# Hybrid decoder step on one core: first gated outputs loaded one unit ahead, branch weights walked forth and back

## Chip, core, metric

One Trainium2 chip, one core of it. The metric is the device time of one execution in microseconds (us), the median of the runs shown. All arithmetic is float32; products are made from two fp32r halves (a high part and the rest).

## What is computed

One layer for a prompt of 2048 positions and a sample group of 8 x 8 positions, D_MODEL 1024. A combined input projection feeds two branches, a windowed attention and a gated linear attention (GLA). The part that matters here is how the branch outputs are joined:

```python
h = rms_norm(x, norm_g) * (1.0 + scale) + shift
q_a, k_a, v_a, z_a, q_g, k_g, v_g, lr_g, z_g, m_a, m_g = split_proj(h @ w_in)
...
o_a = attention(...) * silu(z_a)                     # 512 channels
o_g = rms_norm(gla(...), gla_norm_g) * silu(z_g)     # 512 channels
merged = sigmoid(m_a) * (o_a @ w_branch_att) + sigmoid(m_g) * (o_g @ w_branch_gla)
y = x + gate * (merged @ w_out)
```

## The kernel before

Three phases follow each other. Sixteen prompt tiles of 128 positions and one sample tile of 64 are the units of position; weights and activations have their contraction rows on the 128 partitions, in chunks (`r`, `d`) of 128 rows.

**phase_a1** makes the modulation, the normed input, the attention branch, and stores the attention outputs per tile in DRAM (`oa_dram`).

**phase_gla** (L589) runs the rest of the input projection as 16 weight units `u`, over three blocks of columns `bi` (384, 384 and 288 columns; the loops stand at L920 and L927). A unit loads its raw weights (`raw`, L613, pool `r`, 7 buffers), splits each into halves (`halves`, L606: a cast on ACT, a subtraction on DVE, pool `w`, 7 buffers) and makes 7 products of 12 matmuls (L941) into banks a to d. Between them the GLA steps (`step`, L913) are worked off. In block 1 each unit also splits one piece of the branch weights and stores it in DRAM (`branch_weights`, L652: tile `wl`, store `sw<-wl`). Some units also prepare the *first gated outputs*, those of the first block of the last phase: `first_outputs(zc)` (L896) for eight chunks `zc` of channels. It loads the gate path `z` and four tiles of branch output `or`, takes the sigmoid on ACT (L903), multiplies twice on DVE (L904, L905), splits (`o0w`) and stores (`o<-o0w`, L907). Chunks 0 to 3 stand in units 9, 11, 13 and 15 of block 1, chunks 4 to 7 in units 0 to 3 of block 2; loads and products stand together at the beginning of a unit. `z`, `or` and the sigmoid `sg` are buffers of the pool `r`.

**phase_out** (L965) has four blocks `bi` of tiles: 512, 512, 512 and 576 positions, the last with the sample tile. In each block:

- the gated outputs `o[zc]` (trace name `d_o`) are made for 8 chunks from `z` and `orw` (L1014 to L1026); for block 0 they are loaded ready;
- for each of 8 chunks `dj` of output channels, two gate paths `s` are loaded and put through the sigmoid (L1039 to L1044), two products of 12 matmuls are made (`product`, L580, matmuls at L585, trace name `q`), and DVE joins and splits the result into `m` (L1054 to L1060, `split` L990). Two chunks `dj` share one *branch unit*, 2 MB of split weights, loaded by `unit` (L974) in two halves (`u_b<-sw`, L977) into one of two buffers, even units into `wp0`, odd ones into `wp1`. Units are taken in the order 0, 1, 2, 3 in each block, so each block loads four;
- the output projection: 8 groups of 24 matmuls (L1078, trace name `e`; the sample tile at L60), summed over `r` = 0 to 7 in that order, then gate, residual and store.

In block 0 the output weights `wo` are loaded as well, as 16 pieces (`pieces`, L994, three buffers `x`), each split by ACT and DVE (L991, L992). They are tied behind the branch units on their queue by `issue_after` (L1033).

All these transfers are issued by SP, in one order. The order on each engine and on SP's queue is not the program's: a scheduler fixes it when the program is built, with the program's order as priority and a simulated time line for what is ready (`schedule_with_timeline_sim=True`). At run time each engine and each queue goes strictly in that fixed order. So the last products of one block and the first ones of the next can be mixed on PE.

Of the kernel before, what the change touches and what calls it, by code (L numbers as in the profile page):

```python
# [9 lines left out]
F32R = mybir.dt.float32r  # L10
# [7 lines left out]
P = 128  # L18
D = 1024
NC = 8  # L20
# [16 lines left out]
def f(ap):  # L37
    return ap.bitcast(F32)
# [550 lines left out]
def phase_gla(k, dp):  # L589
# [4 lines left out]
    tc, nc, I, O = k.tc, k.nc, k.i, k.o  # L594
    k.og_dram = {}
    with ExitStack() as es:
# [16 lines left out]
        def raw(name, src=None):  # L613
            r = rp.tile([P, 4, P], F32, tag="r", name=name)
            if src is not None:
                nc.sync.dma_start(r, src)
            return r
# [277 lines left out]

        def first_outputs(zc):  # L896

            z, o, sg = (raw(f"{n}0_{zc}") for n in ("z", "or", "sg"))
            flat = lambda t: t.rearrange("p a b -> p (a b)")
            nc.sync.dma_start(flat(z), zm[zc][:, 0, 0:512])  # L900
            for n, t in enumerate(k.blocks[0]):
                nc.sync.dma_start(o[:, n], (k.oa_dram if zc < 4 else k.og_dram)[t][:, zc % 4])
            nc.scalar.activation(sg, z, AF.Sigmoid)  # L903
            nc.vector.tensor_tensor(z, z, o, op=ALU.mult)  # L904
            nc.vector.tensor_tensor(z, z, sg, op=ALU.mult)  # L905
            k.o0[zc] = dp.tile([P, 2, 512], F32R, tag=f"o0_{zc}", name=f"o0_{zc}")
            nc.sync.dma_start(f(k.o0[zc]), f(halves(z, f"o0w{zc}")).rearrange("p a b c -> p a (b c)"))  # L907

        k.o0 = {}
        lags = ((store, 5), (output, 4), (levels, 3), (operands, 2), (decay, 0), (sums, 1), (fetch, 1))  # L910
        steps = iter(range(len(k.order2) + 5))

        def step():  # L913
            n = next(steps, None)
            for fn, lag in lags if n is not None else ():
                if 0 <= n - lag < len(k.order2):
                    fn(k.order2[n - lag])

        step()
        for bi, (c0, c1) in enumerate(SB):  # L920
            N = c1 - c0
            w, X = unit(bi, 0) if bi == 0 else None, [None] * 7
            for p in ORDER:
                X[p] = xp.tile([P, 2, 4, 384], F32R, tag=f"x{p}", name=f"x{p}_{bi}")[:, :, :, :N]
                nc.sync.dma_start(f(X[p]), f(k.xd[bi][p]))
            at = range(0, 12, 2) if bi < 2 else (0, 1, 2, 4, 5, 6, 8, 9, 10)
            for u in range(16):  # L927
                if u - 4 in at:
                    step()
                if bi == 1:  # L930
                    branch_weights(u)
                if (bi == 1 and u in (9, 11, 13, 15)) or (bi == 2 and u < 4):
                    first_outputs(u // 2 - 4 if bi == 1 else u + 4)
                w = unit(bi, u) if bi or u else w
                bank = {b: ps_d.tile([P, 512], F32, tag=b, name=f"{b}{bi}_{u}")[:, :N] for b in "abcd"}
                oc = [ep.tile([P, 2, 384], F32, tag="oc", name=f"oc{n}_{bi}_{u}")[:, :, :N] for n in range(2)]
                t = [up.tile([P, 384], F32, tag="u", name=f"u{n}_{bi}_{u}")[:, :N] for n in range(3)]
                for p, b, wt in zip(ORDER, "abcdacd", w):
                    for d in range(4):
                        for n, (x, y) in enumerate(((0, 0), (0, 1), (1, 0))):  # L940
                            nc.tensor.matmul(bank[b], wt[:, x, d], X[p][:, y, d], start=(p > 3 or p == 0) and d == 0 and n == 0,  # L941
                                             stop=(d == 3 and n == 2), skip_group_check=True)
                    if p == 0:
                        nc.scalar.copy(t[0], bank["a"])
                    elif p == 5:
                        nc.vector.tensor_tensor(t[0], bank["b"], t[0], op=ALU.add)
                    elif p == 4:
                        nc.scalar.copy(t[1], bank["c"])  # L948
                    elif p == 6:
                        nc.vector.tensor_tensor(t[2], bank["d"], t[0], op=ALU.add)  # L950
                        nc.gpsimd.tensor_tensor(oc[1][:, 1], t[2], t[1], op=ALU.add)  # L951
                    elif p == 1:
                        nc.scalar.copy(oc[0][:, 0], bank["a"])  # L953
                    elif p == 2:
                        nc.vector.tensor_tensor(oc[1][:, 0], bank["c"], t[0], op=ALU.add)
                    else:
                        nc.vector.tensor_tensor(oc[0][:, 1], bank["d"], t[0], op=ALU.add)
                for n in range(2):
                    dst = qkv[2 * u + n] if u < 4 else zm[2 * (u - 4) + n]
                    nc.sync.dma_start(dst[:, :, c0:c1], oc[n])  # L960
# [4 lines left out]
def phase_out(k):  # L965

    tc, nc, I, O = k.tc, k.nc, k.i, k.o
    with ExitStack() as es:
        tp = lambda name, bufs, **kw: es.enter_context(tc.tile_pool(name=name, bufs=bufs, reuse_waits="tile", **kw))

        wop, mp_, wp1, sp, wp0, op = tp("dewo", 1), tp("dem", 1), tp("dew1", 1), tp("des", 2), tp("dew0", 1), tp("deo", 1)
        pse, psl = tp("depa", 3, space=PSUM), tp("depb", 5, space=PSUM)

        def unit(key):  # L974
            w = (wp0, wp1)[int(key[-1]) % 2].tile([P, 2, NC, 256], F32R, tag="w", name="u" + key)
            for n, r in enumerate((slice(0, 4), slice(4, 8))):
                ins = nc.sync.dma_start(f(w[:, :, r]), f(k.split[int(key[-1])][:, :, r]))  # L977
                if key == "0_b0":
                    outputs(4 * n)
            return w[:, 0], w[:, 1], ins  # L980

        def outputs(zc0):

            for zc in range(zc0, zc0 + 4):
                o0.append(op.tile([P, 2, NB], F32R, tag=f"o{zc}", name=f"d_o0_{zc}"))
                last.append(nc.sync.dma_start(f(o0[zc][:, :, :512]), f(k.o0[zc])))
# [17 lines left out]
        for bi in range(len(k.blocks)):  # L1004
# [4 lines left out]
            o = [op.tile([P, 2, NB], F32R, tag=f"o{zc}", name=f"d_o{bi}_{zc}") for zc in range(8)] if bi else o0  # L1009
# [4 lines left out]
            for zc in range(8) if bi else ():  # L1014
                od = k.oa_dram if zc < 4 else k.og_dram
                z = sp.tile([P, NB], F32, tag="z", name=f"z{bi}_{zc}")
# [5 lines left out]
                sg = sp.tile([P, NB], F32, tag="sg", name=f"sg{bi}_{zc}", bufs=1)  # L1022
# [1 line left out]
                nc.vector.tensor_tensor(z[:, :N], z[:, :N], orw[:, :N], op=ALU.mult)  # L1024
                nc.vector.tensor_tensor(sg[:, :N], sg[:, :N], z[:, :N], op=ALU.mult)
                split(o[zc][:, 0, :N], o[zc][:, 1, :N], sg[:, :N])  # L1026
            for dj in range(8):
                if dj % 2 == 0 and (bi or dj):
                    with tc.issue_after(last[-1].ins) if bi == 0 else nullcontext():
                        wb = unit(f"{bi}_b{dj // 2}")  # L1030
                if bi == 0 and dj in (4, 6):
                    for e in (dj - 4, dj - 3):
                        with tc.issue_after(wb[2].ins):  # L1033
                            pieces(wo[:, :, :, e * 256:e * 256 + 256], I["w_o"][e], f"o{e}")
                if bi == 0 and dj == 7:
                    gate = wop.tile([P, D], F32, tag="gate", name="gate")
                    nc.sync.dma_start(gate, k.gates[:P])
                sm = []
                for s in range(2):  # L1039
                    t = sp.tile([P, NB], F32, tag=f"s{s}", name=f"s{s}_{bi}_{dj}")  # L1040
                    for o0, hf, c0, n in at:
                        nc.sync.dma_start(t[:, o0:o0 + n], zm[8 + 2 * dj + s][:, hf, c0:c0 + n])
                    nc.scalar.activation(t[:, :N], t[:, :N], AF.Sigmoid)  # L1043
                    sm.append(t)  # L1044
                sums = []
                for s in range(2):
                    ps = [psl.tile([P, 512], F32, tag="ps", name=f"q{s}{bi}_{dj}_{u}") for u in range(len(spl))]
                    rows = list(range(4 * s, 4 * s + 4))
                    product(nc, ps, spl, wb, dj % 2 * P, rows, o, rows)
                    sums.append(ps)  # L1050
                for u, (s0, s1) in enumerate(spl):
                    n = s1 - s0
                    sa, sg = sm[0][:, s0:s1], sm[1][:, s0:s1]
                    nc.vector.tensor_tensor(sa, sums[0][u][:, :n], sa, op=ALU.mult)  # L1054
                    nc.vector.tensor_tensor(sg, sums[1][u][:, :n], sg, op=ALU.mult)
                    nc.vector.tensor_tensor(sa, sa, sg, op=ALU.add)
                    e = min(s1, np_)
                    split(mp[:, 0, dj, s0:e], mp[:, 1, dj, s0:e], sa[:, :e - s0])
                    if s1 > np_:
                        split(ms[:, dj, 0], ms[:, dj, 1], sa[:, np_ - s0:n])  # L1060
# [196 lines left out]
```

## Time and profile before

| | |
|---|---|
| median of 3 runs | 1628.81 us |
| the runs | 1638.41, 1628.81, 1628.66 us |
| the profiled execution | 1636.97 us, its span 1635.2 us (1.8 us lie around it) |
| mean granted TensorE clock in it | 0.969 |
| DMA | 382.17 MB, mean 234 GB/s |

A span begins and ends with the first and last instruction seen. PE is TensorE's matmuls, PEld its weight loads, DVE VectorE, ACT ScalarE, POOL GpSimd, SPq the queue of the engine that issues the transfers. A granted clock of 1.0 is 2.4 GHz, 0.5 is 1.2 GHz. In a time line the last bracket is the idle time of the engine before the instruction and what ended it.

### The profile page before, as it was taken

What the parts mean: (1) busy time and instruction counts of PE and PEld (TensorE: products, weight loads), DVE (VectorE), ACT (ScalarE), POOL (GpSimd) and SP (SyncE); (2) the same over time, 40 slices, a digit from 0 to 9 for tenths busy, and PEclk for the clock granted to TensorE, in tenths of its full rate; (3) what the DMA queues carried; (4) which work ended last, traced back from release to release, by engine and by line L of the source; (5) the groups of instructions that cost most, each with busy time, mean ns of one, the idle gap of its engine ahead of it and who ended that gap; (6) DMA issues with size and microseconds to landing.
All of it is one profiled execution on the core that took longest, in us unless ns stands there. A gap on an engine that the chain in (4) does not pass through costs nothing.

```text
span 1635.2 us, 26988 instructions
## 1 busy us (share of the span) xinstructions
PE 1547.5 (95%) x9528; PEld 1349.5 (83%) x9528; DVE 1032.7 (63%) x2168; ACT 695.9 (43%) x1618; POOL 467.5 (29%) x553
## 2 busy tenths in 40 slices
PE   7789999989989999999999999999999889999998
PEld 5666666657989999899989998998898568888997
DVE  5886878764586877554666667677562653646452
ACT  3676856644433443333344445454232421313120
POOL 1895774652555444111111111124110000000000
PEclk9988999988999999899999999999999989999999
DMA  9875473566776566999667789966569976876633
GB/s 376 257 229 150 142 254 86 152 211 264 246 249 228 187 211 208 383 302 282 223 218 244 248 284 363 326 198 180 192 227 346 299 236 204 266 241 213 206 113 103
DMA packets 288283, 382.17 MB, mean 234 GB/s; under 512 B 37569, under 2 KB 196178, under 8 KB 284820
## 3 DMA queue, kind: packets, MB, share of 16 engines
q1 hardware_dynamic: 285700, 376.13, 69.7%
q10 hardware_dynamic: 2448, 4.33, 0.7%
q8 instruction: 75, 1.23, 0.3%
q14 instruction: 60, 0.49, 0.1%
HBM read 257.30 MB, written 123.08 MB: 233 GB/s over the span
## 4 chain that ended last, share of the span: by engine, by line
PE 43%; DMA 7%; DVE 5%; ACT 2%; issue 1%; SPq 1%; POOL 0%; ACTq 0%; DVEq 0%; POOLq 0%
PE e L1078 10%; PE q L585 9%; PE c L941 5%; PE d L941 5%; PE a L941 5%; PE b L941 2%; PE g_l L798 2%; DMA wo<-in_w_o 2%; DMA sw<-wl 1%; DVE KQ L750 1%; DMA o<-o0w 1%; DMA u_b<-sw 1%; DVE ATp L804 1%; DVE w L610 1%; DMA s<-zm 1%
## 5 line engine op out<-in xcount | busy, mean ns | idle before, releaser
L610 DVE TENSOR_TENSOR w<-r,w 128x512 fp32r<-128x512 f32 x208 | 158.7, 766 | 100.4 <-ACT w L609 91.4
L941 PE MATMUL c<-x,w 128*128 128x384 f32 (+1 forms) x1152 | 211.2, 329 | 6.5 <-ACT u L948 6.5
L941 PE MATMUL d<-x,w 128*128 128x384 f32 (+1 forms) x1152 | 205.9, 326 | 7.7 <-DVE u L950 7.7
L941 PE MATMUL a<-x,w 128*128 128x384 f32 (+1 forms) x1152 | 207.4, 325 | 0.2 <-ACT oc L953 0.2
L585 PE MATMUL q<-d_o,u_b 128*128 128x512 f32 (+1 forms) x960 | 189.6, 358 | 13.2 <-ACT d_o L991 9.6
L941 PEld LDWEIGHTS c<-x,w 128*128 128x128 f32 x1152 | 189.6, 192 | 11.1 <-ACT u L948 8.8
L941 PEld LDWEIGHTS d<-x,w 128*128 128x128 f32 x1152 | 188.9, 190 | 11.1 <-DVE u L950 8.6
L585 PEld LDWEIGHTS q<-d_o,u_b 128*128 128x128 f32 x960 | 161.3, 191 | 40.5 <-ACT d_o L991 11.6
L609 ACT CAST w<-r 128x512 fp32r<-128x512 f32 x208 | 127.4, 621 | 151.3 <-DMA sw<-wl 40.6
L941 PEld LDWEIGHTS a<-x,w 128*128 128x128 f32 x1152 | 185.5, 188 | 3.5 <-issue 1.3
L1078 PE MATMUL e<-wo,d_m 128*128 128x512 f32 x768 | 177.6, 392 | 2.8 <-ACT wo L991 2.6
L1078 PEld LDWEIGHTS e<-wo,d_m 128*128 128x128 f32 x768 | 144.7, 189 | 34.5 <-ACT wo L991 3.4
L951 POOL TENSOR_TENSOR oc<-u,u 128x384 f32<-128x384 f32 (+1 forms) x48 | 55.9, 1165 | 337.0 <-DVE u L950 169.5
L304 PE MATMUL pd<-whi,hs 128*128 128x512 f32 (+1 forms) x512 | 143.6, 361 | 7.0 <-DVE hs L242 4.3
L304 PEld LDWEIGHTS pd<-whi,hs 128*128 128x128 f32 x512 | 92.4, 196 | 26.2 <-DVE hs L242 4.5
L941 PE MATMUL b<-x,w 128*128 128x384 f32 (+1 forms) x576 | 105.5, 323 | 1.1 <-ACT w L609 1.1
L941 PEld LDWEIGHTS b<-x,w 128*128 128x128 f32 x576 | 93.3, 188 | 1.9 <-ACT w L609 1.4
L304 PE MATMUL pd<-wlo,hs 128*128 128x512 f32 (+1 forms) x256 | 91.7, 360 | 0.0
L375 ACT ACTIVATE sm<-sm,nm,rs 128x256 f32<-128x256 f32 (+1 forms) x128 | 74.5, 587 | 8.2 <-DVE nm L371 7.8
L750 DVE TENSOR_TENSOR KQ<-KQ,M 128x512 f32<-128x512 f32 (+2 forms) x115 | 71.8, 625 | 0.0
L804 DVE COPY_PREDICATED ATp<-maskp,g_l 128x256 f32<-128x256 int32 x112 | 58.4, 522 | 16.6 <-PE g_l L798 14.9
L1043 ACT ACTIVATE s<-s 128x512 f32<-128x512 f32 (+1 forms) x64 | 40.6, 645 | 65.1 <-DMA s<-zm 63.3
(252 smaller groups left out, 2611.4 us busy)
## 6 DMA issues: line engine op xcount, KB each, us to landing
r<-in_w_x SPq DMA_DIRECT2D x160, 256.0 KB
w<-tx SPq DMA_DIRECT2D x64, 512.0 KB
u_b<-sw SPq DMA_DIRECT2D x32, 1024.0 KB
x<-xd SPq DMA_DIRECT2D x14, 1536.0 KB
zm<-oc SPq DMA_DIRECT2D x48, 384.0 KB
xd<-sx SPq DMA_DIRECT2D x32, 512.0 KB
tx<-w SPq DMA_DIRECT2D x32, 512.0 KB
r<-tw SPq DMA_DIRECT2D x64, 256.0 KB
```

What stands on the lines that cost most here:

```text
L304: nc.tensor.matmul(pd[u][:T, :hi - lo], hs[:, d // 4, a, d % 4, :T], (whi, wlo)[b][:, d, lo:hi], start=(d == 0 and n == 0), stop=(d == NC ...
L375: nc.scalar.activation(sm[:, h, :w], sm[:, h, :w], AF.Exp, scale=0.125 if rq is None else rs[:, h:h + 1], bias=nm[:, h:h + 1], accum_out=d ...
L585: nc.tensor.matmul(ps[u][:, :s1 - s0], w[a][:, r, cs:cs + P], x[xr[n0]][:, b, s0:s1], start=(n0 == 0 and n == 0), stop=(n0 == len(rows) - ...
L609: nc.scalar.copy(w[:, 0], src)
L610: nc.vector.tensor_tensor(w[:, 1], src, f(w[:, 0]), op=ALU.subtract)
L750: nc.vector.tensor_tensor(out.rearrange("p a (n m) -> p a n m", m=m), x.rearrange("p a (n m) -> p a n m", m=m), M[r, b, at[n]:at[n + 1]].u ...
L798: nc.tensor.matmul(pl[:T, r, j, l - l0, :H], KQ[rr, l, j] if l else c["kT"][rr, j, :T], KQ[rr, l, 2 + j].rearrange("p (n s m) -> p n s m", ...
L804: nc.vector.copy_predicated(g.AT[:T].rearrange("p h (n s m) -> p h n s m", s=2, m=m)[:, :, :, 1, :], g.mask[:T, l, :].rearrange("p (n m) - ...
L941: nc.tensor.matmul(bank[b], wt[:, x, d], X[p][:, y, d], start=(p > 3 or p == 0) and d == 0 and n == 0, stop=(d == 3 and n == 2), skip_grou ...
L951: nc.gpsimd.tensor_tensor(oc[1][:, 1], t[2], t[1], op=ALU.add)
L1043: nc.scalar.activation(t[:, :N], t[:, :N], AF.Sigmoid)
L1078: nc.tensor.matmul(ps, mp[:, a, r, o0:o0 + T], wo[:, b, r, cs], start=(r == 0 and n == 0), stop=(r == 7 and n == 2))
```

## The change

First outputs become a generator: the loads of a chunk are issued in units 8, 10, 12, 14 of block 1 and 0 to 3 of block 2, its products follow in the next unit. So chunks 0 to 3 load one unit sooner and are multiplied where they were, and chunks 4 to 7 load where they did and are multiplied one unit later. In phase_out `unit` remembers what each of the two buffers holds and hands it out again; even blocks take `dj` as 0, 1, ... 7, odd blocks as 6, 7, 4, 5, 2, 3, 0, 1.

```diff
@@ -895,18 +895,20 @@
 
         def first_outputs(zc):
 
-            z, o, sg = (raw(f"{n}0_{zc}") for n in ("z", "or", "sg"))
+            z, o = (raw(f"{n}0_{zc}") for n in ("z", "or"))
             flat = lambda t: t.rearrange("p a b -> p (a b)")
             nc.sync.dma_start(flat(z), zm[zc][:, 0, 0:512])
             for n, t in enumerate(k.blocks[0]):
                 nc.sync.dma_start(o[:, n], (k.oa_dram if zc < 4 else k.og_dram)[t][:, zc % 4])
+            yield
+            sg = raw(f"sg0_{zc}")
             nc.scalar.activation(sg, z, AF.Sigmoid)
             nc.vector.tensor_tensor(z, z, o, op=ALU.mult)
             nc.vector.tensor_tensor(z, z, sg, op=ALU.mult)
             k.o0[zc] = dp.tile([P, 2, 512], F32R, tag=f"o0_{zc}", name=f"o0_{zc}")
             nc.sync.dma_start(f(k.o0[zc]), f(halves(z, f"o0w{zc}")).rearrange("p a b c -> p a (b c)"))
 
-        k.o0 = {}
+        k.o0, outs = {}, {}
         lags = ((store, 5), (output, 4), (levels, 3), (operands, 2), (decay, 0), (sums, 1), (fetch, 1))
         steps = iter(range(len(k.order2) + 5))
 
@@ -929,8 +931,11 @@
                     step()
                 if bi == 1:
                     branch_weights(u)
-                if (bi == 1 and u in (9, 11, 13, 15)) or (bi == 2 and u < 4):
-                    first_outputs(u // 2 - 4 if bi == 1 else u + 4)
+
+                for n in (u - 1, u):
+                    if (bi == 1 and n in (8, 10, 12, 14)) or (bi == 2 and n in (0, 1, 2, 3)):
+                        zc = n // 2 - 4 if bi == 1 else n + 4
+                        next(outs.setdefault(zc, first_outputs(zc)), None)
                 w = unit(bi, u) if bi or u else w
                 bank = {b: ps_d.tile([P, 512], F32, tag=b, name=f"{b}{bi}_{u}")[:, :N] for b in "abcd"}
                 oc = [ep.tile([P, 2, 384], F32, tag="oc", name=f"oc{n}_{bi}_{u}")[:, :, :N] for n in range(2)]
@@ -971,13 +976,19 @@
         wop, mp_, wp1, sp, wp0, op = tp("dewo", 1), tp("dem", 1), tp("dew1", 1), tp("des", 2), tp("dew0", 1), tp("deo", 1)
         pse, psl = tp("depa", 3, space=PSUM), tp("depb", 5, space=PSUM)
 
+        held = {}
+
         def unit(key):
-            w = (wp0, wp1)[int(key[-1]) % 2].tile([P, 2, NC, 256], F32R, tag="w", name="u" + key)
-            for n, r in enumerate((slice(0, 4), slice(4, 8))):
-                ins = nc.sync.dma_start(f(w[:, :, r]), f(k.split[int(key[-1])][:, :, r]))
+            n = int(key[-1])
+            if held.get(n % 2, (None,))[0] == n:
+                return held[n % 2][1]
+            w = (wp0, wp1)[n % 2].tile([P, 2, NC, 256], F32R, tag="w", name="u" + key)
+            for h, r in enumerate((slice(0, 4), slice(4, 8))):
+                ins = nc.sync.dma_start(f(w[:, :, r]), f(k.split[n][:, :, r]))
                 if key == "0_b0":
-                    outputs(4 * n)
-            return w[:, 0], w[:, 1], ins
+                    outputs(4 * h)
+            held[n % 2] = n, (w[:, 0], w[:, 1], ins)
+            return held[n % 2][1]
 
         def outputs(zc0):
 
@@ -1024,7 +1035,9 @@
                 nc.vector.tensor_tensor(z[:, :N], z[:, :N], orw[:, :N], op=ALU.mult)
                 nc.vector.tensor_tensor(sg[:, :N], sg[:, :N], z[:, :N], op=ALU.mult)
                 split(o[zc][:, 0, :N], o[zc][:, 1, :N], sg[:, :N])
-            for dj in range(8):
+
+            for n in range(8):
+                dj = (n // 2 if bi % 2 == 0 else 3 - n // 2) * 2 + n % 2
                 if dj % 2 == 0 and (bi or dj):
                     with tc.issue_after(last[-1].ins) if bi == 0 else nullcontext():
                         wb = unit(f"{bi}_b{dj // 2}")
```

## Rows read from the trace of the kernel before

**Rows 1.** Page: busy time and share of the span, by engine

```profile
PE 1547.5 (95%) x9528; PEld 1349.5 (83%) x9528; DVE 1032.7 (63%) x2168; ACT 695.9 (43%) x1618; POOL 467.5 (29%) x553
```

**Rows 2.** Windows: stretch, length, busy us (count) per engine, PEclk, DMA share, GB/s

```profile
1243.10:1282.51 39.41, 36.76 (x158) 29.23 (x158) 14.85 (x24) 12.77 (x20) 0.00 (x0) 1.00 0.97 327
1282.51:1323.78 41.27, 28.49 (x92) 19.98 (x92) 28.44 (x45) 20.74 (x36) 0.00 (x0) 0.75 0.90 291
1441.81:1485.33 43.52, 43.52 (x193) 36.04 (x193) 22.32 (x33) 12.34 (x20) 0.00 (x0) 1.00 0.79 264
800.00:960.00 160.00, 151.50 (x1052) 144.35 (x1051) 103.22 (x215) 76.66 (x161) 25.26 (x29) 1.00 0.77 245
```

**Rows 3.** Chain of waits, 1230 to 1330 us: start, length, what

```profile
1283.28 11.43 DMA u_b<-sw
...
1299.36 8.90 DMA wo<-in_w_o
...
1308.32 7.00 DMA s<-zm
```

**Rows 4.** Waits of PE, 1280 to 1325 us: total, times, longest

```profile
PE q L585 <- ACT d_o L991: 9.6, 3, 3.8
PE e L1078 <- ACT wo L991: 2.6, 2, 1.7
```

**Rows 5.** DMA issues over the whole span: count, KB each

```profile
u_b<-sw SPq DMA_DIRECT2D x32, 1024.0 KB
```

**Rows 6.** Time line of SP's queue, 1195 to 1335 us

```profile
1282.70 1.18 SPq L977 DMA_DIRECT2D u_b<-sw  x2
1283.97 3.06 SPq L998 DMA_DIRECT2D wo<-in_w_o  x3
...
1307.61 0.52 SPq L977 DMA_DIRECT2D u_b<-sw  x1
...
1320.13 0.38 SPq L998 DMA_DIRECT2D wo<-in_w_o  x1
```

**Rows 7.** Time line of PE, 960 to 1000 us: the first unit of block 2

```profile
984.37 1.12 PE L823 MATMUL g_s<-g_v,kd 128*64 128x128 f32 x8 [2.01 <-ACT g_oT L891]
985.43 2.40 PE L798 MATMUL g_l<-KQ 64*128 64x64 f32 x20
...
988.52 2.94 PE L941 MATMUL c<-x,w 128*128 128x288 f32 x12
...
993.09 1.33 PE L798 MATMUL g_l<-KQ 64*128 64x64 f32 x18
...
997.34 1.84 PE L941 MATMUL c<-x,w 128*128 128x288 f32 x12
```

**Rows 8.** Waits of ACT, 640 to 1240 us

```profile
ACT w L609 <- DMA sw<-wl: 40.6, 10, 6.4
...
ACT L903 <- DMA z<-zm: 5.2, 1, 5.2
```

**Rows 9.** Waits of PE, 800 to 1240 us

```profile
PE c L941 <- ACT u L948: 5.8, 6, 1.8
```

**Rows 10.** Time line at the end of the last block's products

```profile
1579.84 6.53 PE L60 MATMUL e<-wo,d_m 128*128 128x512 f32 x28
...
1579.91 0.82 DVE L1055 TENSOR_TENSOR s<-q,s 128x288 f32<-128x288 f32 x2 [2.38 <-PE q L585]
...
1581.65 0.90 DVE L992 TENSOR_TENSOR d_m<-s,d_m 128x288 fp32r<-128x288 f32 x3 [0.19 <-ACT d_m L991]
```

**Rows 11.** Chain of waits of the whole span: a raw weight load; a unit's products

```profile
973.54 9.47 DMA r<-in_w_x
...
1000.76 1.58 PE b L941 x12
```

**Rows 12.** Page, groups: the two steps that free a raw buffer

```profile
L610 DVE TENSOR_TENSOR w<-r,w 128x512 fp32r<-128x512 f32 x208 | 158.7, 766 | 100.4 <-ACT w L609 91.4
...
L609 ACT CAST w<-r 128x512 fp32r<-128x512 f32 x208 | 127.4, 621 | 151.3 <-DMA sw<-wl 40.6
```

## Prediction

> **What bounds the kernel now.** I read the page first, then windows over the whole span, then the chain of waits and the waits of PE where a window showed PE idle. PE is busy 95% of the span, DVE 63% [rows 1]; so PE sets the end, and an edit is worth what it takes out of the 88 us in which PE is idle (1635.2 - 1547.5), or out of the time in which PE runs at the lower clock. Two of the places that the change touches have such losses.
>
> The first is the passage into the last phase. In a stretch without any loss 192 matmuls take 43.52 us, 0.2267 us each (the row counts 193, with one cut by its edge) [rows 2]. From 1282.51 to 1323.78 us PE makes only 92 in 41.27 us [rows 2]. At 0.2267 they are 20.9 us, so 20.4 us are lost: 12.8 idle (41.27 - 28.49) and 7.6 to a granted clock of 0.75 over the stretch, a mixture of its two levels that comes with the idle time. In the 39.41 us before it 158 matmuls would take 35.8, a loss of 3.6. In both stretches the DMA share is 0.90 to 0.97, at 291 and 327 GB/s: the transfers are the limit, not DVE (28.44 of 41.27) [rows 2]. The chain of waits goes through them: 11.43 us for a branch unit, 8.90 for a piece of `wo`, 7.00 for a gate path [rows 3]. PE itself waits for operands of block 1 (9.6 us) and for split pieces of `wo` (2.6) [rows 4]. After 1324 us it runs without a gap to the tail.
>
> The second is the first outputs. In block 1's half from 800 to 960 us PE is idle 8.5 us (160.00 - 151.50) [rows 2]; at the first unit of block 2 one wait of 2.01 us is followed by a spell at the lower clock [rows 7].
>
> **The change, part by part.** *Branch units kept.* Before, four units of two halves in each of four blocks make 32 loads of 1024 KB [rows 5]. After, blocks 1 to 3 find the two units that they begin with in place and load two: 8 + 3 x 4 = 20 loads. Of the twelve that go, eight belong to the starts of blocks 2 and 3, and there PE has no gap to give (as in the stretch at 1441.81, clock 1.00, DMA 0.79 [rows 2]): nothing gained. Four, the loads of block 1's first two units, are issued from 1282.70 to 1307.61 us [rows 6], inside the stretch that loses. They are 4.19 MB; at its 291 GB/s that is 14.4 us of a queue that is nearly full. The chain holds one of them with 11.43 us [rows 3]. The gain can't be more than the 20.4 us lost there. From below: the ten last pieces of `wo`, issued from 1283.97 to 1320.13 us [rows 6], go through three buffers, each with a landing, a cast and a subtraction, and these steps stay; if that cycle is what holds PE, only the transfers' competition goes, and it may be nothing. I take 12, next to the row of the chain, a little under the bytes' 14.4, because something is late next: the pieces of `wo`, then block 1's `d_o`.
>
> By the Trainium skill, page "DMA: Bandwidth & Descriptors", section "Anatomy of one DMA", a transfer costs about 2.0 us fixed (measured there for the software-generated path) plus its bytes at 436 GB/s: an estimate of 2.6 us for a piece of 256 KB. The trace has 8.90 us for one [rows 3], so most of it would be queueing, which the change removes; by that rule the pieces would stop being late, which is the second rival below.
>
> *Odd blocks backwards.* The number of products is the same. But the output projection sums over `r` from 0, and in blocks 1 and 3 the chunks 0 and 1 now come last, so it meets the fresh result at its second step, where before it had 28 matmuls (6.53 us in the last block) of older chunks to make first [rows 10]. The result of the last chunk is ready 2.64 us after the products end (1579.91 to 1581.65 + 0.90) [rows 10]. What still covers it are the `r` = 0 matmuls of the three groups that have a PSUM buffer: in block 3 two groups of the sample tile with 2 and one of 3, 7 x 0.2267 = 1.6 us, so 1.0 is exposed. In block 1, three groups of 3 give 2.0 us; nearly all is covered. Bounds: 0 and 2.64 in each. I take +1 in all.
>
> *First outputs.* No instruction is added; loads and products are set apart. At the first unit of block 2 ACT stood 5.2 us before the sigmoid until `z` had landed [rows 8], behind it in ACT's queue waited the copy `g_oT`, and PE waited 2.01 us for that. Then 20 matmuls took 2.40 us, where later 18 took 1.33, and 12 took 2.94 against 1.84 [rows 7]; PE lost 2.0 + 0.9 + 1.1 = 4.0 us there. With the sigmoid one unit later `z` has long landed. What is late next is the raw weights under a full DMA; I take 3 of the 4. In block 1 PE waited six times, 5.8 us, for ACT's copy `u` [rows 9]; ACT was held by casts that wait until a store of `wl` has landed (ten times, up to 6.4 us) [rows 8]. These stores share the DMA engines with the loads of `z` and `or`, issued right behind them; the change moves those loads to the unit before, next to that unit's store. The wait moves with them: I take 0, between -5.8 (all gone) and +5.8 (once more in the even units). The new distance costs buffers: a pair `z`, `or` holds two of seven raw buffers for one unit more. Below I price that as a rival; its cover is the slack of the other five.
>
> **The sum.** -12 - 3 + 1 = -14 us. Made against the profiled execution, 1636.97 us, it gives 1623.0. The median of the runs is 8.2 us lower, 1628.81, and the loss in it may be smaller where the clock is lost; I take the same difference: 1614.8, predicted as 1615 us.
>
> **The rivals.**
> - *The passage stays bound by the cycle of pieces and operands.* For it: PE waits for `d_o` and `wo`, never for a branch unit [rows 4]. Against: the 11.43 us of a branch unit in the chain, the DMA share of 0.90. Then 3 us come from the passage: -3 - 3 + 1 = -5, 1623.8.
> - *The passage loses nothing any more.* For it: the landing of 8.90 us for 256 KB [rows 3], the clock of 0.75 that would come back with the gaps [rows 2]. Against: DVE still has 28.44 us of work in the stretch, and the block's operands need the old ones free. -20.4 - 4.0 + 1 = -23.4, 1605.4.
> - *Slower: raw buffers run short in units 1 to 3 of block 2*, where the pair of one chunk is still held while the next is loaded: four of seven. A raw weight takes 9.47 us to land under a full DMA [rows 11], then 0.62 for the cast and 0.77 for the subtraction [rows 12], 10.9 us a buffer. A unit needs five and has 7 x 1.58 = 11.1 us of products [rows 11]. Seven buffers give 5/7 x 10.9 = 7.8 us, five 10.9, three 18.2: 7.1 us late, and with 2.0 us of lower clock as after the wait in [rows 7] 9.1 in each of three units, +27. With -12 + 1: +16, 1645. It outweighs the gain as soon as it strikes in more than one unit (11 / 9.1 = 1.2). Against it: the products of a chunk free its pair early in the unit, so that three is the worst moment, not the rule.
> - That the change doesn't do what it says I can exclude: which units are kept is settled when the program is built.
>
> **Chances.** The forecast 0.42, with 1608 to 1621 as its own range; the first rival 0.24, the second 0.27, the slower one 0.07. About 1% (16.3 us) is what a measurement tells from no change here. Faster than 1612.5 are the second rival and a quarter of the forecast: 0.36; slower than 1645.1 is most of the last: 0.05; 0.59 remain. The range of 1601 to 1629 reaches over the second rival, with the waits of block 1 gone too (1605 - 5), down to 1601, and up to no gain at all.
>
> **What would show it.** Right: 20 loads `u_b`; no `u_b` in the chain between the first products of the last phase and the steady stretch; that passage (92 matmuls in 41.27 us before) shorter by some 12 us, at a clock near 1.0; no wait of ACT for `z` before a sigmoid. The reversed blocks: a wait of PE of about 1 us before the second row of the sample tile's sums. Wrong: the passage as long as before with PE waiting for `wo` or `d_o`; loads `r` waiting for free buffers and ACT's casts waiting for `r` in units 1 to 3 of block 2; or new gaps of several us elsewhere, since a scheduler orders all queues anew from the first changed instruction on.

## The result and the profile after

The changed kernel takes 1615.66 us (1613.29 to 1617.14, 4 runs) against 1630.39 us of the kernel before (4 runs), a ratio of 0.9899 with a 95% interval of 0.9862 to 0.9936: 10 to 22 us less. 1615 us was predicted, from a median before of 1628.81.

The profiled executions differ by more, 1635.2 against 1615.4 us of span. To see where, I cut both at the same instructions: the first product of phase_gla, the first one of its block 2, the first product `q` of the last phase, and the 481st `q`, which is the middle of that phase's block 2.

| stretch | before | after | difference |
|---|---|---|---|
| start to the first product of phase_gla | 381.7 | 375.2 | -6.5 |
| to the first of its block 2 | 594.2 | 595.6 | +1.4 |
| to the first `q` | 267.2 | 264.9 | -2.3 |
| to the 481st `q` (the *passage*) | 220.3 | 207.2 | -13.1 |
| to the end | 171.8 | 172.5 | +0.7 |

The first row is code that the change doesn't touch, and in the fourteen kernels profiled here it varied from 373.1 to 381.7 us. So this one pair of profiles holds 6.5 us that belong to no edit, about as much as the profiled execution of before (1636.97) lay above the median. An effect of a few us can't be read from one pair; what follows rests on the timed runs and on stretches compared over many kernels. The ratios leave out two slow runs, one of e3 with 1882.51 us and one of e6 with 1662.70, whose mean granted clock was 0.745 and 0.864.

The windows of the kernel before (stretch, length, busy us and count of PE, PEld, DVE, ACT, POOL, then PEclk, DMA share, GB/s):

```profile
975.90:1243.10 267.20, 259.71 (x2124) 248.19 (x2125) 167.65 (x359) 109.76 (x258) 52.95 (x62) 0.96 0.78 258
1243.10:1463.40 220.30, 204.87 (x864) 164.83 (x865) 113.49 (x174) 64.83 (x107) 0.00 (x0) 0.95 0.79 256
```

The same of the changed kernel, and two more that answer to [rows 2]:

```profile
970.80:1235.70 264.90, 256.29 (x2127) 243.28 (x2125) 165.49 (x358) 111.15 (x259) 51.90 (x62) 0.98 0.79 260
1235.70:1442.90 207.20, 199.63 (x864) 162.79 (x865) 113.90 (x174) 65.62 (x108) 0.00 (x0) 0.99 0.73 233
...
1235.70:1275.08 39.38, 36.29 (x156) 29.05 (x156) 14.10 (x22) 12.21 (x19) 0.00 (x0) 1.00 0.98 323
1275.08:1316.55 41.47, 37.22 (x154) 29.85 (x155) 32.41 (x51) 21.82 (x38) 0.00 (x0) 0.96 0.76 239
```

The stretch from 1275.08 us answers to the one in which 92 matmuls took 41.27 us [rows 2]. Now 154 fit into 41.47 us; at 0.2267 us each they are 34.9, so 6.6 us are lost where 20.4 were. The clock is 0.96 where it was 0.75, and the DMA share 0.76 where it was 0.90: there the queue is no longer full. In the 39.38 us before it the share is 0.98, as full as before. Of the 13.1 us that the whole passage gained, 7.9 are idle time of PE (220.30 - 204.87 = 15.43 before, 207.20 - 199.63 = 7.57 after) and 5.2 busy time, with a clock of 0.99 for 0.95.

The chain of waits of the changed kernel through that stretch (start, length, what) holds no branch unit; pieces of `wo` stand in it, and they land in less than half the time once the queue has emptied:

```profile
1264.55 10.00 DMA wo<-in_w_o
...
1283.41 3.96 DMA wo<-in_w_o
...
1288.77 3.65 DMA wo<-in_w_o
```

Waits of PE in the changed kernel, 1270 to 1330 us (total, times, longest): `wo` is what is late now.

```profile
PE e L1091 <- ACT wo L1002: 5.0, 2, 3.9
PE e L1091 <- DVE wo L1003: 0.2, 1, 0.2
```

Its issues of branch units over the span, where [rows 5] had 32:

```profile
u_b<-sw SPq DMA_DIRECT2D x20, 1024.0 KB
```

At the first unit of block 2 the waits of ACT (955 to 1005 us) name no `z` any more, where [rows 8] had 5.2 us:

```profile
ACT u L953 <- PE c L946: 4.2, 1, 4.2
ACT w L609 <- DMA r<-in_w_x: 4.0, 2, 3.2
```

and the time line of PE there shows waits for operands, after which the clock did not fall: 16 matmuls `g_l` take 1.06 us, where 20 took 2.40 [rows 7].

```profile
977.63 1.81 PE L946 MATMUL c<-x,w 128*128 128x288 f32 x12 [1.71 <-DMA w<-tx]
...
980.90 1.06 PE L798 MATMUL g_l<-KQ 64*128 64x64 f32 x16
...
986.18 1.85 PE L946 MATMUL a<-x,w 128*128 128x288 f32 x12 [0.81 <-DMA x<-xd]
```

### The profile page after: what moved, and what is told of

The parts are those of the page before. It is cut to its first block, busy times and chain, and to the rows that moved or that the text cites. A ratio compares the mean times of both kernels' runs of the same rounds, so it can differ in the third digit from the quotient of the medians.

```text
span 1615.4 us, 26971 instructions
## 1 busy us (share of the span) xinstructions
PE 1536.5 (95%) x9528; PEld 1340.7 (83%) x9528; DVE 1035.4 (64%) x2168; ACT 697.3 (43%) x1619; POOL 465.9 (29%) x553
## 4 chain that ended last, share of the span: by engine, by line
PE 44%; DMA 7%; DVE 4%; ACT 2%; issue 1%; SPq 0%; POOL 0%; ACTq 0%; DVEq 0%; POOLq 0%
PE e L1091 10%; PE q L585 6%; PE d L946 6%; PE a L946 6%; PE c L946 6%; PE b L946 3%; DMA s<-zm 3%; PE g_l L798 2%; DMA wo<-in_w_o 1%; DMA w<-tx 1%; DMA r<-in_w_x 1%; PE g_o L818 1%; PE g_o L819 1%; PE g_o L853 1%; DVE ATp L804 1%
## 5 line engine op out<-in xcount | busy, mean ns | idle before, releaser
L946 PE MATMUL d<-x,w 128*128 128x384 f32 (+1 forms) x1152 | 206.7, 327 | 8.8 <-DVE u L955 8.3
L585 PE MATMUL q<-d_o,u_b 128*128 128x512 f32 (+1 forms) x960 | 184.9, 352 | 2.9 <-DVE s L1067 1.3
L610 DVE TENSOR_TENSOR w<-t,w 128x512 fp32r<-128x512 f32 x64 | 59.4, 939 | 16.9 <-ACT w L609 15.4
```

The lines of the kernel that those rows point to most:

```text
L585: nc.tensor.matmul(ps[u][:, :s1 - s0], w[a][:, r, cs:cs + P], x[xr[n0]][:, b, s0:s1], start=(n0 == 0 and n == 0), stop=(n0 == len(rows) - ...
L610: nc.vector.tensor_tensor(w[:, 1], src, f(w[:, 0]), op=ALU.subtract)
```

## The experiments

**The two parts apart.** The new last phase with the old first outputs, and the other way round:

```diff
 e1:  phase_gla as before, phase_out as changed
 e2:  phase_gla as changed, phase_out as before
```

> The last phase as changed (two branch units kept, odd blocks backwards), the first outputs as before. Theory A (the gain is that of the 4.19 MB that are not loaded in the passage into the last phase): nearly the whole gain, a ratio of 0.991 to 0.994 (10 to 14 us faster than before), 20 loads of branch units, and no branch unit in the chain after the first products. Theory B (the two parts give about half each): 0.995.

> The first outputs loaded one unit ahead, the last phase as before. Theory A: 0 to 3 us faster (0.998 to 1.0), the wait of ACT for z before the first unit of block 2 gone, the six or so waits of PE for ACT's copy u still there, only in other units; the passage loses its 20 us as before. Theory B: 6 to 8 us faster (0.995 to 0.996), as the two profiled executions seem to say, where the first products of the last phase start 7.4 us sooner.

Measured: e1 0.9941 (0.9918 to 0.9964), 9.6 us faster than before; e2 0.9955 (0.9934 to 0.9976), 7.3 us faster. Together they are 16.9 us, within the whole's 10 to 22. Neither theory had both: e1 is nearly what A said (10 to 14 us), e2 is what B said (6 to 8), where A gave 0 to 3. Windows of e1, then of e2 (block 2 of phase_gla, and the passage):

```profile
973.50:1241.20 267.70, 259.78 (x2124) 248.03 (x2124) 167.88 (x359) 109.44 (x258) 53.26 (x62) 0.96 0.78 256
1241.20:1449.00 207.80, 200.54 (x865) 163.59 (x865) 113.79 (x174) 65.47 (x108) 0.00 (x0) 0.98 0.73 231
```

```profile
972.90:1233.50 260.60, 251.78 (x2126) 239.43 (x2125) 167.03 (x358) 110.96 (x259) 51.77 (x62) 1.00 0.79 264
1233.50:1448.60 215.10, 203.43 (x865) 163.78 (x866) 113.96 (x174) 66.18 (x108) 0.00 (x0) 0.97 0.81 263
```

Each part shortens its own stretch: the passage is 207.8 us in e1, as in the whole change, and block 2 is 260.6 us in e2 and unchanged in e1 (267.7). That e2's passage is 5 us under the 220.3 of before, without a unit kept, stays open; it is one execution, with a clock of 0.97 against 0.95. So in the profiles keeping the units is worth 12.5 us of passage with the old first outputs (220.3 to 207.8) and 7.9 with the new ones (215.1 to 207.2).

**Is it the bytes?** e3 keeps the new order and loads every unit again, with the first outputs as before (its edit is shown against the last phase as changed). e7 leaves the change and puts the bytes back, as transfers whose data nothing uses; e10 puts back half of them, e11 twice as many. In the cut of e7, `wo_ins` is the list of the loads of the pieces of `wo`; the lines that fill it are left out.

```diff
 e3:
-            if held.get(n % 2, (None,))[0] == n:
-                return held[n % 2][1]
 e7 (e10: unit 3 alone; e11: each twice):
             if held.get(n % 2, (None,))[0] == n:
+                for h, r in enumerate((slice(0, 4), slice(4, 8))) if key[0] == "1" else ():
+                    extra = k.dp.tile([P, 2, 4, 256], F32R, tag=f"ex{key}{h}", name=f"ex{key}{h}")
+                    with tc.issue_after(wo_ins[5 if n == 3 else 9 + h].ins):
+                        nc.sync.dma_start(f(extra), f(k.split[n][:, :, r]))
                 return held[n % 2][1]
```

> Odd blocks backwards, but every unit loaded again, 32 loads as before (first outputs as before too). Theory A (bytes): the passage is as long as before or longer, 0.998 to 1.006 of before. Theory C (the new order lets the scheduler mix the products better, the bytes do nothing): as fast as the kept units, 0.991 to 0.994.

> The changed kernel with four extra transfers of 1 MB, DRAM to DRAM, that nothing waits for, put on SP's queue among the pieces of wo where block 1's units were loaded before. Theory A (bytes in a full queue): the passage from the first product to the steady stretch grows by 9 to 14 us against the changed kernel, the whole is back within 4 us of before. Theory C (waits of the queue for buffers, or the order, not bytes): within 3 us of the changed kernel.

> The changed kernel with two extra transfers of 1 MB in the passage, where the earlier run had four and its passage was 12.5 us longer. If each byte in the full queue costs its time: the passage 5 to 8 us longer than the changed kernel's 207.2 us. If it was a threshold, or the place of the later two: under 3 or over 10.

> The changed kernel with eight extra transfers of 1 MB in the passage. If each byte costs its time: the passage 22 to 30 us longer than the changed kernel's. If the first four had filled what slack there was, or PE's other work covers more: under 18.

Measured: e3 1.0074 (1.0052 to 1.0097), slower than before; e7 0.9966 (0.9949 to 0.9983); e10 0.9943 (0.9918 to 0.9968); e11 1.0050 (1.0023 to 1.0078). The passages, in this order:

```profile
1238.10:1460.00 221.90, 202.98 (x864) 163.88 (x865) 112.94 (x174) 65.42 (x108) 0.00 (x0) 0.97 0.78 255
```

```profile
1230.60:1450.30 219.70, 204.11 (x865) 165.24 (x866) 113.92 (x174) 65.32 (x108) 0.00 (x0) 0.96 0.75 239
```

```profile
1232.40:1448.30 215.90, 203.34 (x864) 164.92 (x865) 113.59 (x174) 65.65 (x108) 0.00 (x0) 0.97 0.73 233
```

```profile
1228.60:1459.30 230.70, 205.97 (x864) 165.58 (x865) 114.07 (x174) 65.80 (x108) 0.00 (x0) 0.93 0.76 245
```

The new order with every unit loaded gives nothing (221.9 against 220.3 of before), and e7, which has the new order and the kept units, is nearly as long as before: theory C falls. 4.19 MB back make the passage 12.5 us longer than the changed kernel's 207.2, nearly the 13.1 that taking them away had saved; twice as many make it 23.5 us longer, 2.1 MB 8.7. So the passage pays about 3 us for each MB, with more for the first two MB (8.7 us lies between the two cases that were expected, 5 to 8 and over 10); the clock falls with the bytes too, from 0.99 to 0.93. The timed runs agree: by the difference of the ratios from 0.9899, 2.1, 4.19 and 8.4 MB cost some 7, 11 and 25 us. That e7 as a whole stays 5.5 us under before (0.34%), where within 4 was expected, fits the gain of the other part, which it keeps.

Two things limit this. The extra transfers don't stand quite where the loads stood: the first two are issued 31 us after the first `q`, where the DMA share was 0.98 without them; before, the first two loads of block 1 were issued after 39.6. And though nothing uses their data, SP itself waits for them: it holds back its next transfers until an extra one has landed. Waits of SP's queue in e7 (1228 to 1330 us; total, times, longest):

```profile
SPq L1060 <- DMA ex_b<-sw: 5.5, 2, 3.2
...
SPq L1013 <- DMA ex_b<-sw: 2.1, 1, 2.1
```

So the runs show that bytes in SP's queue cost this much, but not how the cost divides between sharing the DMA engines and holding back SP's next issue. The same bytes issued from another engine's queue would tell; that was not run.

e3 (expected 0.998 to 1.006) came out a little slower than that. One reason shows: an odd block now begins with the unit used last, whose buffer comes free late. The 193rd `q`, the first of block 1, comes 62.6 us after the first, where before it came after 50.5, and PE waits 1.9 us there for a branch unit. But its profiled passage is only 1.6 us longer than before, and its timed runs are 12 us slower; where the rest lies is open.

**Do the other eight loads matter?** e6 keeps units only from block 0 to block 1.

```diff
-            if held.get(n % 2, (None,))[0] == n:
+            if key[0] == "1" and held.get(n % 2, (None,))[0] == n:
...
-                dj = (n // 2 if bi % 2 == 0 else 3 - n // 2) * 2 + n % 2
+                dj = (n // 2 if bi == 0 else 3 - n // 2) * 2 + n % 2
```

> The changed kernel, but units are kept only from block 0 to block 1; blocks 1 to 3 all go backwards and blocks 2 and 3 load all four units, 28 loads of branch units instead of 20. If the eight loads at the starts of blocks 2 and 3 are worth nothing, as the prediction says: as fast as the changed kernel, within 2 us. If a fuller queue costs something there: 3 us slower or more.

Measured: 0.9895 (0.9875 to 0.9916), the ratio of the changed kernel, with 28 loads. The eight loads at the starts of blocks 2 and 3 are worth nothing that the timed runs can tell, as predicted. Its one profile has 209.1 us for the passage and 173.4 to the end, 1.9 and 0.9 us more than the changed kernel, so a cost of 2 or 3 us is not excluded.

**Which first outputs?** e8 and e9 put loads and products together again, for one half of the chunks each.

```diff
 e8 (added lines only):
+                if bi == 1 and u in (9, 11, 13, 15):
+                    for _ in first_outputs(u // 2 - 4):
+                        pass
 e9 (added lines only):
+                if bi == 2 and u < 4:
+                    for _ in first_outputs(u + 4):
+                        pass
```

> The changed kernel, but chunks 0 to 3 of the first outputs are loaded and multiplied together again in units 9, 11, 13, 15 of block 1; chunks 4 to 7 stay as changed. Theory A (the gain of the first outputs lies at the beginning of block 2, where the sigmoid waited for z): as fast as the changed kernel, 0.988 to 0.992 of before. Theory B (it lies in block 1, where DVE waited for or): 4 to 7 us of it lost, 0.993 to 0.995.

> The changed kernel, but chunks 4 to 7 are loaded and multiplied together again in units 0 to 3 of block 2; chunks 0 to 3 stay as changed. Theory A: 4 to 7 us lost against the changed kernel, 0.993 to 0.995 of before, with ACT again waiting some 5 us for z in front of a sigmoid and PE 2 to 3 us for the copy g_oT at the first unit of block 2. Theory B: as fast as the changed kernel, 0.988 to 0.992.

Measured: e8 0.9900 (0.9880 to 0.9919), e9 0.9940 (0.9915 to 0.9965). Theory A holds: chunks 0 to 3 gain nothing, chunks 4 to 7 all of it. In e9 the stall is back. The waits of ACT, 960 to 1010 us, then the time line of PE, then the window of block 2:

```profile
ACT L905 <- DMA z<-zm: 3.7, 1, 3.7
```

```profile
984.73 0.76 PE L823 MATMUL g_s<-g_v,kd 128*64 128x128 f32 x8 [1.94 <-ACT g_oT L891]
```

```profile
976.40:1244.50 268.10, 259.61 (x2126) 247.90 (x2124) 169.61 (x359) 109.24 (x257) 52.32 (x62) 0.96 0.77 256
```

**What is late next?** e5 gives the pieces of `wo` a fourth buffer. e12 is the changed kernel once more, and e13 is e5 and e8 together.

```diff
 e5 (all three tiles of this tag):
-                t = sp.tile([P, 2, 256], F32, tag="x", name=f"w{name}_{r}", bufs=3)
+                t = sp.tile([P, 2, 256], F32, tag="x", name=f"w{name}_{r}", bufs=4)
```

> The changed kernel with four buffers instead of three for the pieces of wo (and for the rows of x later on). Theory A (what is late next in the passage is the cycle of three buffers): PE's 5 us of waiting for split pieces gone, 3 to 6 us faster than the changed kernel, 0.986 to 0.988 of before. Rival (the pieces are late because the queue is full): no change, within 2 us of the changed kernel.

> The changed kernel once more, to stand beside the next one on the same chip: 0.988 to 0.993 of before. Its profile says how much the stretches of the first one vary: the passage 206 to 209 us, the stretch from the first product of block 2 to the first product of the last phase 260 to 266 us.

> Four buffers for the pieces of wo, and chunks 0 to 3 of the first outputs loaded and multiplied together again. Each alone was 2 to 3 us under the changed kernel, which no interval tells apart. If both are real: 4 to 6 us faster than the changed kernel. If they are not: within 2 us of it.

Measured: e5 0.9881 (0.9858 to 0.9904), 1612.41 us; e12 0.9908 (0.9874 to 0.9941), 1614.60 us; e13 0.9902 (0.9869 to 0.9935), 1612.54 us. In e5 PE doesn't wait for `wo` any more, but for other things (waits of PE, 780 to 1330 us):

```profile
PE q L585 <- DVE s L1068: 2.5, 2, 2.1
PE q L585 <- ACT d_o L1002: 1.9, 1, 1.9
...
PE q L585 <- DVE s L1067: 1.5, 1, 1.5
```

Its passage is 206.1 us and e13's 205.8, where e12 has 206.7. The wait moved rather than went, and no version is told apart from the changed kernel by its interval: e5 lies short of the 3 to 6 us that theory A expected, and e13 is 2.1 us under e12, near the case in which neither gain is real.

## Why the prediction was right

*The passage, -12 predicted.* e1, which is this term with the reversal, measures -9.6 (-5.9 to -13.4); in the profiles the passage shrank by 7.9 to 13.1, and it grew by 12.5 when the bytes came back. The reason given, bytes in a queue that is nearly full, is shown by e1, e7, e10 and e11, with the limit said there. The pieces of `wo` were late next (5.0 us), as the working assumed, though e5 gains nothing that can be measured by taking that wait away. The two rivals for this place bracket the result: had only the cycle of pieces bound it, the passage would have gained some 3 us; had nothing been late any more, the 6.6 us left would be gone.

By the Trainium skill (page "DMA: Bandwidth & Descriptors", section "Anatomy of one DMA") a piece of 256 KB would cost an estimated 2.6 us, by a fit to transfers of the software-generated path. The trace has 8.90 us before; after the change it has 10.00 at the start of the passage, where the queue is still full, and 3.65 to 3.96 behind it. So most of the 8.90 was queueing, but the pieces did not stop being late.

*The eight other loads, 0 predicted.* e6 agrees, to within 2 or 3 us.

*The reversal, +1 predicted.* The mechanism is right and the size a little too large. The predicted wait was for the fresh chunk at the second step of the sums, covered by seven `r` = 0 matmuls. The time line of PE and of its weight loads at the end of block 3 of the changed kernel:

```profile
1559.38 1.09 PE L60 MATMUL e<-wo,d_m 128*128 128x512 f32 x4
...
1560.31 5.98 PE L1091 MATMUL e<-wo,d_m 128*128 128x512 f32 x24
...
1561.21 0.30 PEld L1091 LDWEIGHTS e<-wo,d_m 128*128 128x128 f32 x2 [0.48 <-ACT d_m L1002]
1561.70 4.17 PEld L1091 LDWEIGHTS e<-wo,d_m 128*128 128x128 f32 x19 [0.20 <-DVE d_m L1003]
...
1566.13 6.51 PE L60 MATMUL e<-wo,d_m 128*128 128x512 f32 x28
```

`d_m` is what the weight loads bring in, so the wait stands with them and not with the matmuls. After the four `r` = 0 matmuls of the sample tile and three of a prompt tile, the load for the prompt tile's second row waits 0.48 us for the cast of the fresh chunk, and the one behind it 0.20 us for the subtraction. The 28 matmuls up to 1566.13 take 6.75 us; at 0.2267 they are 6.35, so PE lost 0.4 us. The same two waits, 0.5 and 0.2 us, stand in the last stretch of every profiled kernel with the reversal, and in neither of the two without it. The sum had 2.64 - 1.6 = 1.0 us, because it let the sums wait until all parts of the fresh chunk were split; the scheduler put the rows of the prompt tile in front, whose part is split first. At block 1 the cover was the nine `r` = 0 matmuls that were counted, and three matmuls of the next block behind them, so that no wait for `d_m` is left:

```profile
1377.57 2.20 PE L1091 MATMUL e<-wo,d_m 128*128 128x512 f32 x9
1379.75 0.49 PE L585 MATMUL q<-d_o,u_b 128*128 128x512 f32 x1
1380.47 0.73 PE L585 MATMUL q<-d_o,u_b 128*128 128x512 f32 x2 [0.23 <-DVE d_o L1003]
```

The stretch behind the passage takes 172.1 to 172.5 us in the kernels with the reversal (173.4 in e6) and 171.8 in the two without.

*The first outputs, -3 predicted.* The place is right and shown by e9: the sigmoid that waited for `z`, the copy `g_oT` behind it, PE's wait. The size is not: e2 measures -7.3 (-3.9 to -10.8). The step that failed is "PE lost 2.0 + 0.9 + 1.1 = 4.0 us there", of which I took 3 and so counted half as idle time. It priced the first unit alone. Block 2 of phase_gla takes 260.5 to 266.4 us in the ten profiled kernels with chunks 4 to 7 set apart (mean 263.0) and 267.2 to 271.9 in the four without (mean 268.7): 5.7 us less, without an overlap. But PE is idle no less: 9.2 us on average (263.0 less 253.8 busy) against 8.2 (268.7 less 260.5). The 2.0 us before `g_s` went, and waits of 1.71, 0.81 and less for operands came. What the stretch gained is busy time, 6.7 us for the same 2124 to 2127 matmuls, and with it goes the granted clock, 0.97 to 1.00 in the one group, 0.95 to 0.96 in the other. Windows show where. Counted from the first product of block 2, the kernel before has four spells at the lower clock, in the first 20 us, from 90 us, from 160 and from 200; below it, the same four windows of the changed kernel:

```profile
975.90:995.90 20.00, 17.99 (x143) 17.02 (x143) 10.11 (x20) 6.67 (x19) 2.66 (x3) 0.83 1.07 393
1065.90:1075.90 10.00, 9.79 (x83) 9.06 (x83) 4.98 (x12) 5.08 (x16) 2.59 (x4) 0.83 0.68 191
1135.90:1145.90 10.00, 9.40 (x67) 8.25 (x67) 6.34 (x14) 2.23 (x6) 5.91 (x8) 0.83 0.55 170
1175.90:1185.90 10.00, 7.77 (x48) 7.45 (x48) 6.72 (x16) 1.54 (x3) 1.10 (x1) 0.66 0.50 173
```

```profile
970.80:990.80 20.00, 16.62 (x142) 15.15 (x141) 9.29 (x20) 6.85 (x18) 3.44 (x4) 1.00 1.08 392
1060.80:1070.80 10.00, 10.00 (x96) 9.35 (x95) 7.45 (x19) 4.22 (x10) 2.61 (x4) 1.00 0.74 196
1130.80:1140.80 10.00, 10.00 (x62) 8.39 (x61) 5.25 (x10) 2.09 (x6) 5.50 (x8) 0.66 0.60 192
1170.80:1180.80 10.00, 8.74 (x66) 7.91 (x65) 8.21 (x18) 3.38 (x7) 1.10 (x1) 0.83 0.75 240
```

The first two spells are gone in all ten kernels with these chunks set apart and stand in all four without. The last two stand in all four as well, but only in some of the ten: both in the changed kernel and e5, one of them in e7, e10 and e12, neither in e2, e6, e8, e11 and e13; e11 and e12 have another some 40 us in. So the forecast priced one spell out of four. What makes the clock fall is not shown, and the length of a wait alone doesn't decide it: in e8 a wait of 1.95 us stands at the first unit with the clock at 1.00, while the waits of 2.01 us before and of 1.94 in e9 were followed by the lower clock.

```profile
977.56 1.81 PE L948 MATMUL c<-x,w 128*128 128x288 f32 x12 [1.95 <-DMA w<-tx]
```

Why the second spell went too, and why the last two come and go, is open. For block 1 I took 0 because the wait would move from odd to even units, and e8 agrees: setting chunks 0 to 3 apart changes nothing.

*The slower rival* did not come: in the first units of block 2 ACT waited 4.0 us for raw weights where before it waited 0.6, so the shortage it named left a trace, but far from the 7.1 us in each of three units.

The forecast gave the first outputs 4 us too little, which lies outside the interval of e2, and the passage with the reversal about 1 us too much, which lies well inside that of e1. That the sum, -14, came so near the measured -14.7 is partly luck.

## What to carry to other kernels

Price a transfer that is taken away by the bytes it takes out of a stretch in which the queue is full and the bounding engine waits: 4 of the 12 loads removed here made the gain of their part, and the other 8 nothing that the timed runs tell. A wait in front of one instruction of an in-order engine is to be priced with all that queues behind it and with PE's clock, over the whole stretch that the new order reaches: here the clock was worth more than the wait. And look for a predicted stall in the weight loads as well as in the matmuls.

## What had not been expected

The part up to the first product of phase_gla, the same program in all, took from 373.1 to 381.7 us in the fourteen profiled executions, a spread about as large as either part of the change is worth. The gain of the first outputs came with no less idle time of PE, but with a higher clock. And bytes that nothing uses cost as much as loads that are needed, about 3 us per MB; SP's queue waits for them all the same.
